# The sparse and the stick-breaking attention take their four query blocks from the last to the first

## The chip, the cores and the metric

The kernel runs on one core of one Trainium2 chip, as one launch. The metric is device time in microseconds (us). Engines are named as the profile names them: PE is TensorE's matrix unit, PEld its weight load, DVE VectorE, ACT ScalarE, POOL GpSimd, SP the queue that issues the weight loads from memory.

## The reference, cut to what matters

Two stacks of two transformer layers run one after the other over 512 tokens of width 1024. The second stack is the one concerned. Each of its layers mixes tokens in three ways, projects the joined result back to width 1024, and goes through a feed-forward part.

```
o_gdn = gated_deltanet(...)                 # a scan over chunks of 64 tokens
o_nsa = native_sparse_attention(...)        # 6 heads: compressed + selected + window
o_sb  = stick_breaking_attention(q, k, v)   # 4 heads
mix = concat([o_gdn, norm(o_nsa), norm(o_sb)])
h = h + mix @ w_out
```

Both attentions are causal and run over four query blocks of 128 tokens. Block b sees the keys of blocks 0 to b, so its score tiles are 128(b+1) wide: block 0 has the smallest tiles, block 3 the largest. The blocks don't depend on each other. With 512 tokens all eight selection blocks of 64 keys are chosen and the window reaches back over everything, so the selected and the windowed part are both plain causal attention, over different keys and values. In the stick-breaking attention a weight is sigmoid(z) times the product of sigmoid(-z) over the keys behind it.

## The kernel before, in words

All products of a projection are made of three fp32r products (high x high, high x low, low x high), so PE carries far more than any other engine. A weight tile comes from memory on SP's queue (L266), ACT copies its high part (`whi`, L278) and DVE subtracts (`wlo`, L279).

Inside a mixing stage `drive` fixes PE's order by hand while the program is built. One generator, `main`, makes the projections. Side generators (`spawn`, `begin`, `crew`) make everything else. Each yields the time, on a planned clock that counts PE's columns, at which its next products may stand; a priority and a share decide who goes next. Every product is then chained to the one before it, so PE keeps this order whatever happens on the chip. The other engines' order comes from a scheduler that places instructions by a timeline of its own. Each engine then runs its list in order.

What matters for the change, in `block2_mix`:

- `nsa` yields jobs in an order given by its loop over b: `compressed(b)`, then 6 heads on the selected keys (`vs`), then 6 heads on the window (`vw`). A crew of 4 workers (`LIVE[2]`) takes them one by one.
- A head (`head`, L705 on) is: score products (`k`,`kl` with `q`, and the causal mask) into a PSUM bank; maximum `nm` on DVE; exponential `e` on ACT; transposes of `e` on PE; a copy `et` on ACT or DVE; products with the values into `ps_o`.
- After 6 heads `add_part` scales the sum (`no`, DVE) and adds it on POOL (`on`). After the third part `head_norm` follows: square `hsq` on ACT, a sum and a scale `hv` on DVE, a power on POOL, the product `on` on DVE.
- When the crew is through, `mark("nsa")` stands 8.62 planned us later. Then `mix_features` transposes `on` (12 transposes) and splits it into `hi` (ACT) and `lo` (DVE), which gives `mix1`.
- `main` goes on meanwhile with the projections `z1`, `sq`, `sk`, `sv`, and then waits for `mix0` (from the delta-rule scan) and `mix1` before `out_proj(mixa)`, 144 products of 512 columns.
- `breaking` turns `sq` and `sk` into transposed halves: 8 + 8 transposes, 4 copies `q` and 8 copies `k` on ACT, as many subtractions `q` and `kl` on DVE. It then starts `stick`, a crew of 4 over four blocks of 4 heads. A head there is scores, two sigmoids `sn` and `sg` on ACT, a scan `rest` on DVE, a product `sg` on DVE, transposes, `et`, products with `sv`.
- In the first layer of the stack `main` also broadcasts a scale (`dgh`, `dgl`, `rb`) at the same spot.

```
for b in range(4):                       # L1909, nsa
    yield compressed(b)
...
for b in range(4):                       # L1978, stick
```

Of the kernel before, what the change touches and what calls it, by code (L numbers as in the profile page):

```python
# [289 lines left out]
def build(ctx, tc, a, out, off, stages=99):  # L290
# [24 lines left out]
    def tmp(shape, name, tag="tmp", dt=F):  # L315
        return slot.tile(shape, dt, tag=tag, name=name, bufs=BUFS[tag])

    def ty(shape, name):
        return tiny.tile(shape, F, tag=f"ty{int(np.prod(shape[1:]))}", name=name)
# [16 lines left out]
    def act(out, in_, func=ACTF.Copy, **kw):  # L336
        ins = nc.scalar.activation(out=out, in_=in_, func=func, **kw).ins  # L337
        kind = SETS.get(func)
        if kind is None:
            return  # L340
        if kind != run_["set"]:
            run_["before"] = [i.name for i in run_["now"]]
            run_["set"], run_["now"], run_["first"] = kind, [], ins
            for name in run_["before"]:
                tc.add_manual_dep(ins, name, NOSYNC, reason="one table set after another")
        else:
            tc.add_manual_dep(ins, run_["first"].name, NOSYNC, reason="one table set after another")
        run_["now"].append(ins)

    def tt(out, in0, in1, op):  # L350
        return nc.vector.tensor_tensor(out=out, in0=in0, in1=in1, op=op)  # L351
# [4 lines left out]
    def ts(out, in0, s1, s2=None, op0=ALU.mult, op1=None):  # L356
        if s2 is None:
            return nc.vector.tensor_scalar(out=out, in0=in0, scalar1=s1, scalar2=None, op0=op0)
        return nc.vector.tensor_scalar(out=out, in0=in0, scalar1=s1, scalar2=s2, op0=op0, op1=op1)
# [43 lines left out]
    def mark(name, lag=0.0):  # L403
        marks[name] = pe["t"] + lag
# [253 lines left out]
    def heads(t, h):  # L658
        return t.rearrange("p (h d) -> p h d", h=h)
# [41 lines left out]
    def scores(q, k, i, b, n):  # L701

        return tuple((q[i][:, blk(b)], part[i][:, 0:n]) for part in k)

    def head(b, weigh, v, out, lag):  # L705

        yield after(0, "s")
        e = weigh()
        yield after(lag[0] + lag[1] * b, "t")
        tp = ps("t", 1.2 + 0.3 * b)  # L710
        for j in range(b + 1):
            tr(tp[:, blk(j)], e[:, blk(j)])
        et = tmp([128, 128 * (b + 1)], "et")
        nc.any.tensor_copy(out=et, in_=tp[:, 0:128 * (b + 1)])
        yield lag[2] + lag[3] * b
        room = after(0, "o")
        yield lambda: room() or not out.fresh()
        o, done = out()
        for j in range(b + 1):
            mm_narrow(o, et[:, blk(j)], v(j), j == 0, j == b)  # L720
        done()
        yield

    def softmax(b, qk, ssum, mask=None):

        n = 128 * (b + 1)
        sp = ps("s", 1.6 + 0.6 * b)
        for i, (q, k) in enumerate(qk):
            mm(sp[:, 0:n], q, k, i == 0, False)
        if mask is None:  # L730
            mm(sp[:, blk(b)], identb, trib, False, True)
        else:
            mm(sp[:, 0:n], identb, mask, False, True)
        nm = ty([128, 1], "nm")
        reduce(nm, sp[:, 0:n], ALU.max, negate=True)
        e = tmp([128, n], "e")
        act(e, sp[:, 0:n], ACTF.Exp, bias=nm, accum_out=ssum)
        return e

    def group(n, finish):  # L740

        st = {"left": n}

        def place(i):
            def out():
                if st["left"] == n:
                    st["o"] = ps("o", np.inf)
                    st["room"] = rooms["o"][-1]
                st["left"] -= 1
                return st["o"][:, 64 * i:64 * i + 64], last if st["left"] == 0 else lambda: None  # L750

            out.fresh = lambda: st["left"] == n
            return out

        def last():
            finish(st["o"])
            st["room"][0] = pe["t"] + 1.5

        return [place(i) for i in range(n)]
# [570 lines left out]
    def block2_mix(l, st, nxt, shared):  # L1330
# [529 lines left out]
        def add_part(b, o, factor):  # L1860
            o, factor = heads(o[:, 0:384], 6), factor.unsqueeze(2).to_broadcast([128, 6, 64])
            if on[b] is None:
                on[b] = sl([128, 6, 64], "on")
                tt(on[b], o, factor, ALU.mult)
            else:
                t = tmp([128, 6, 64], "no")
                tt(t, o, factor, ALU.mult)
                gt(on[b], on[b], t, ALU.add)
            parts[b] += 1
            if parts[b] == 3:  # L1870
                tt(on[b], on[b], head_norm(on[b], 6), ALU.mult)
# [34 lines left out]
            yield  # L1906

        def nsa():
            for b in range(4):  # L1909
                yield compressed(b)  # L1910
                for c, (kk, v) in enumerate(((kh["ks"], vs), (kh["kw"], vw))):
                    ssum = ty([128, 6], "ssum6")

                    def finish(o, b=b, c=c, ssum=ssum):
                        ts(ssum, ssum, 1e-30, op0=ALU.max)
                        nc.vector.reciprocal(out=ssum, in_=ssum)
                        tt(ssum, ssum, sig[:, b, 6 * c + 6:6 * c + 12], ALU.mult)
                        with tc.high_priority():
                            add_part(b, o, ssum)

                    for i2, out in enumerate(group(6, finish)):
                        zz = slice(64 * (i2 % 2), 64 * (i2 % 2) + 64)
                        yield head(b, lambda b=b, i2=i2, kk=kk, ssum=ssum: softmax(b, scores(nqh[i2 // 2], kk, i2 % 2, b, 128 * (b + 1)), ssum[:, i2:i2 + 1]),
                                   lambda jj, v=v, zz=zz: v[:, jj, zz], out, LAG[2])
            mark("nsa_weights")

        def sparse():
            yield until("ks", "kw", "nq0", "nq1", "nq2", "vs", "cmp_k", "cmp_v")
            crew(LIVE[2], nsa(), "nsa", lag=8.62)
            yield until("nsa")  # L1930
            yield from mix_features(on, 1)
# [43 lines left out]
            return sg  # L1975

        def stick():
            for b in range(4):  # L1978
                def finish(o, b=b):
                    t = tmp([128, 4, 64], "sbt")  # L1980
                    act(t, heads(o[:, 0:256], 4))
                    tt(heads(ob[b], 4), t, head_norm(t, 4), ALU.mult)

                for h, out in enumerate(group(4, finish)):
                    yield head(b, lambda b=b, h=h: weigh(b, h), lambda jj, h=h: sv[h // 2][:, jj, 64 * (h % 2):64 * (h % 2) + 64], out, LAG[3])
# [211 lines left out]
```

## Time and profile before

| | us |
|---|---|
| median of 3 runs | 3046.4 |
| the runs | 3045.38, 3050.75, 3046.40 |
| the profiled execution | 3048.71 |
| its span on the core | 3046.9 |
| PE busy in it | 2961.4 (97%) |

The profiled execution lies 2.3 us above the median, and its span 1.8 us below its own time. All times of day below are us from the start of the span. The two mixing stages of the second stack, where the change lies, run from about 1360 to 1780 and from about 2210 to 2620. The sparse attention runs there from 1546 to 1680 in the first of these layers, and ends at 2522 in the second; the stick-breaking attention follows it.

### The profile page before, as it was taken

How to read it: one execution, taken by the hardware profiler on the slowest of the kernel's cores; microseconds unless marked ns; L12 is line 12 of the kernel's file. 1: busy time of each engine (PE TensorE's matmuls, PEld its weight loads, DVE VectorE, ACT ScalarE, POOL GpSimd, SP SyncE). 2: the span in 40 equal slices, each digit the busy share in tenths (PEclk: the TensorE clock that was granted, in tenths of full speed). 3: DMA queues.
4: the chain of work that ended last, by engine and by line, in shares of the span. 5: the costliest groups of instructions: out<-in, count | busy, mean ns of one | idle time of the engine just before them, and what ended most of it. 6: DMA issues, size and time to landing. Idle time of an engine off the chain costs nothing.

```text
span 3046.9 us, 46920 instructions
## 1 busy us (share of the span) xinstructions
PE 2961.4 (97%) x18306; PEld 2471.1 (81%) x18306; DVE 1884.5 (62%) x3426; ACT 1362.9 (45%) x2542; POOL 714.9 (23%) x874
## 2 busy tenths in 40 slices
PE   8999999999999999999999999999999998999998
PEld 7888788888887888888888778887788987788876
DVE  6858444447858434457866675555678666755556
ACT  5654422234645422245455553335454565433353
POOL 4211311123201311145313120002454131200024
PEclk9999999999999999999999999999999999999999
DMA  3212333332222333332310222232323102222322
GB/s 130 82 45 68 90 95 93 96 118 85 68 71 74 96 97 92 95 120 73 94 54 21 81 91 91 95 106 90 116 77 84 63 24 80 92 92 95 106 90 76
DMA packets 105791, 259.38 MB, mean 85 GB/s; under 512 B 21728, under 2 KB 40033, under 8 KB 105569
## 3 DMA queue, kind: packets, MB, share of 16 engines
q1 hardware_dynamic: 97504, 241.70, 25.6%
q10 hardware_dynamic: 8064, 14.68, 1.4%
q8 instruction: 144, 2.36, 0.3%
q14 instruction: 79, 0.64, 0.1%
HBM read 242.84 MB, written 13.50 MB: 84 GB/s over the span
## 4 chain that ended last, share of the span: by engine, by line
PE 45%; DVE 5%; ACT 2%; issue 1%; POOL 1%; DMA 1%; SPq 0%; DVEq 0%; ACTq 0%; POOLq 0%
PE ps_g L382 36%; PE ps_s L382 5%; PE ps_s L392 2%; PE ps_o L388 2%; DVE wlo L279 1%; DVE conv L362 1%; PE ps_s L388 1%; POOL ru L354 1%; ACT whi L278 1%; DVE kl L351 0%; DVE inv L365 0%; ACT L337 0%; DVE pr L351 0%; DVE lo L362 0%; DVE x L351 0%
## 5 line engine op out<-in xcount | busy, mean ns | idle before, releaser
L382 PE MATMUL ps_g<-hi,whi 128*128 128x512 f32 x2768 | 1097.5, 397 | 9.4 <-DVE x L351 3.9
L382 PE MATMUL ps_g<-lo,whi 128*128 128x512 f32 x2768 | 1094.4, 395 | 6.4 <-DVE lo L362 5.8
L382 PE MATMUL ps_g<-hi,wlo 128*128 128x512 f32 x2768 | 1095.5, 396 | 0.0
L278 ACT ACTIVATE whi<-wraw 128x1024 fp32r<-128x1024 f32 (+3 forms) x442 | 458.0, 1036 | 863.3 <-PE ps_g L382 609.5
L279 DVE TENSOR_TENSOR wlo<-wraw,whi 128x1024 fp32r<-128x1024 f32 (+3 forms) x442 | 547.0, 1238 | 252.1 <-ACT whi L278 249.1
L382 PEld LDWEIGHTS ps_g<-hi,whi 128*128 128x128 f32 x2768 | 522.1, 189 | 132.8 <-DVE x L351 6.0
L382 PEld LDWEIGHTS ps_g<-lo,whi 128*128 128x128 f32 x2768 | 522.7, 189 | 127.8 <-DVE lo L362 7.5
L382 PEld LDWEIGHTS ps_g<-hi,wlo 128*128 128x128 f32 x2768 | 522.0, 189 | 115.1
L382 PE MATMUL ps_g<-whi,hi 128*128 128x256 f32 (+4 forms) x1232 | 379.3, 310 | 10.0 <-ACT whi L278 9.1
L382 PE MATMUL ps_g<-whi,lo 128*128 128x256 f32 (+4 forms) x1232 | 347.2, 284 | 3.2 <-DVE lo L362 3.2
L382 PE MATMUL ps_g<-wlo,hi 128*128 128x256 f32 (+4 forms) x1232 | 347.2, 284 | 0.7 <-DVE wlo L279 0.7
L382 PEld LDWEIGHTS ps_g<-whi,hi 128*128 128x128 f32 (+1 forms) x1232 | 232.7, 189 | 26.5 <-ACT whi L278 9.5
L382 PEld LDWEIGHTS ps_g<-whi,lo 128*128 128x128 f32 (+1 forms) x1232 | 231.3, 188 | 5.8 <-DVE lo L362 4.2
L382 PEld LDWEIGHTS ps_g<-wlo,hi 128*128 128x128 f32 (+1 forms) x1232 | 232.5, 189 | 2.6 <-DVE wlo L279 1.0
L354 POOL TENSOR_TENSOR sq<-sq 128x512 f32<-128x512 f32 x102 | 159.9, 1567 | 266.8 <-ACT sq L337 247.9
L354 POOL TENSOR_TENSOR relu<-relu 128x512 f32<-128x512 f32 x64 | 100.9, 1577 | 506.5 <-ACT relu L337 506.5
L362 DVE SCALAR_TENSOR_TENSOR conv<-cv,small,conv 128x512 f32<-128x512 f32 x230 | 186.8, 816 | 5.8 <-ACT conv L337 2.3
L351 DVE TENSOR_TENSOR cv<-ps_g,rb 128x512 f32<-128x512 f32 x106 | 72.8, 690 | 142.8 <-PE ps_g L382 142.7
L351 DVE TENSOR_TENSOR x<-ps_g,x 128x512 f32<-128x512 f32 x112 | 76.9, 688 | 131.6 <-PE ps_g L382 130.9
L337 ACT ACTIVATE e<-ps_s,nm 128x128 f32<-128x128 f32 (+3 forms) x192 | 100.5, 526 | 106.3 <-DVE nm L365 103.2
L351 DVE TENSOR_TENSOR ff<-ps_g,rb 128x512 f32<-128x512 f32 x64 | 44.3, 692 | 162.8 <-PE ps_g L382 162.8
L365 DVE TENSOR_REDUCE nm<-ps_s 128x1 f32<-128x128 f32 (+3 forms) x192 | 91.8, 486 | 80.9 <-PE ps_s L382 78.9
(435 smaller groups left out, 3622.5 us busy)
## 6 DMA issues: line engine op xcount, KB each, us to landing
wraw<-in_w_ff SPq DMA_DIRECT2D x128, 512.0 KB, 3.6
wraw<-in_w_up SPq DMA_DIRECT2D x88, 512.0 KB, 3.4
wraw<-in_w_down SPq DMA_DIRECT2D x32, 448.0 KB, 3.2
wraw<-in_w_out SPq DMA_DIRECT2D x20, 512.0 KB, 3.7
wraw<-in_w_g SPq DMA_DIRECT2D x18, 512.0 KB, 3.5
wraw<-in_w_down SPq DMA_DIRECT2D x16, 512.0 KB, 3.4
wraw<-in_w_pg SPq DMA_DIRECT2D x16, 512.0 KB, 3.4
wraw<-in_w_cq SPq DMA_DIRECT2D x12, 512.0 KB, 3.4
```

What stands on the lines that cost most here:

```text
L278: self.nc.scalar.activation(out=hi, in_=t, func=ACTF.Copy)
L279: self.nc.vector.tensor_tensor(out=lo, in0=t, in1=hi, op=ALU.subtract)
L337: ins = nc.scalar.activation(out=out, in_=in_, func=func, **kw).ins
L351: return nc.vector.tensor_tensor(out=out, in0=in0, in1=in1, op=op)
L354: return nc.gpsimd.tensor_tensor(out=out, in0=in0, in1=in1, op=op)
L362: return nc.vector.scalar_tensor_tensor(out=out, in0=in0, scalar=scalar, in1=in1, op0=op0, op1=op1)
L365: return nc.vector.tensor_reduce(out=out, in_=in_, axis=AX.X, op=op, negate=negate)
L382: placed(nc.tensor.matmul(out=out, lhsT=lhsT, rhs=rhs, start=start, stop=stop).ins, n)
L388: placed(nc.tensor.matmul(out=out[z], lhsT=lhsT[:, z], rhs=rhs, start=start, stop=stop).ins, n)
L392: placed(nc.tensor.transpose(out=out, in_=in_, identity=ident[0:n, 0:n]).ins, 256)
```

## The change

Both loops over the query blocks run 3, 2, 1, 0 instead of 0, 1, 2, 3. Nothing else is edited. The same instructions are issued on each engine, with the same shapes; since PE's order and the other engines' lists are made from the order of the jobs, about 1,100 rows of PE's list stand otherwise in each of the two layers.

```diff
         def nsa():
-            for b in range(4):
+
+            for b in (3, 2, 1, 0):
                 yield compressed(b)
...
         def stick():
-            for b in range(4):
+
+            for b in (3, 2, 1, 0):
                 def finish(o, b=b):
```

Place 1: PE at the end of the sparse attention, first layer of the stack. `ps_g<-whi,hi` and its two neighbours are products of a projection, `ps_g<-hi,whi` those of `out_proj`, `vw,et` the last step of a head of the window part, `on` the transposes that `out_proj` waits for. Before, from the last projection product on (24 such products stand between the last head and the broadcast):

```order
L382 MATMUL ps_g<-whi,hi 128x256
L382 MATMUL ps_g<-wlo,hi 128x256
L382 MATMUL ps_g<-whi,lo 128x256
L382 MATMUL ps_s<-dgh,ones_r 128x512
L382 MATMUL ps_s<-dgl,ones_r 128x512
L392 MATMUL ps_s<-const_105,sq 128x128 x8
L392 MATMUL ps_s<-const_105,sk 128x128 x8
L392 MATMUL ps_s<-const_105,on 128x128 x12
L382 MATMUL ps_g<-hi,whi 128x512
L382 MATMUL ps_g<-lo,whi 128x512
L382 MATMUL ps_g<-hi,wlo 128x512
```

Now, again from the last projection product on:

```order
L382 MATMUL ps_g<-whi,lo 128x256
L392 MATMUL ps_s<-const_105,e 128x128
L382 MATMUL ps_s<-dgh,ones_r 128x512
L382 MATMUL ps_s<-dgl,ones_r 128x512
L392 MATMUL ps_s<-const_105,sq 128x128 x8
L392 MATMUL ps_s<-const_105,sk 128x128 x8
L388 MATMUL ps_o<-vw,et 64x64 x2
L382 MATMUL ps_s<-k,q 128x128
L382 MATMUL ps_s<-kl,q 128x128
L382 LDWEIGHTS identb
L382 MATMUL ps_s<-mskb,identb 128x128
L388 MATMUL ps_o<-vw,et 64x64 x2
```

The projections now end before the sparse attention does. Behind these rows follow the transposes and value products of the heads of block 0 that are still open (6 value steps and 2 scores in all), then the scores of the first four stick-breaking heads (8 products of 512 columns), the 12 transposes of `on`, 8 transposes of `sg`, three products of `out_proj`, 4 more transposes of `sg`, and the first product with `sv`. In the second layer it stands the same way, without the broadcast and with 9 products of `out_proj` ahead of the first product with `sv`.

Place 2: ACT at the same spot (`sv` is the last copy out of a projection, `q` and `k` the copies of the transposed halves). Before:

```order
L337 ACTIVATE sv<-ps_g,rmix 128x128 x4
L337 ACTIVATE hsq<-on 128x384
L337 ACTIVATE dgh<-const_105,rf 128x128 x4
L337 ACTIVATE sv<-ps_g,rmix 128x128
L278 ACTIVATE whi<-wraw 128x768
L337 ACTIVATE sv<-ps_g,rmix 128x128 x3
L337 ACTIVATE rb<-ps_s 128x512
L337 ACTIVATE q<-ps_s 64x512 x4
L337 ACTIVATE k<-ps_s 64x512 x8
```

Now:

```order
L337 ACTIVATE sv<-ps_g,rmix 128x128
L278 ACTIVATE whi<-wraw 128x768
L337 ACTIVATE sv<-ps_g,rmix 128x128 x3
L337 ACTIVATE dgh<-const_105,rf 128x128 x4
L337 ACTIVATE rb<-ps_s 128x512
L337 ACTIVATE q<-ps_s 64x512 x4
L337 ACTIVATE k<-ps_s 64x512 x4
L337 ACTIVATE e,ssum_17010<-ps_s,nm 128x128
L714 COPY et<-ps_s 128x128
L337 ACTIVATE k<-ps_s 64x512 x4
L337 ACTIVATE e,ssum_17010<-ps_s,nm 128x128
L714 COPY et<-ps_s 128x128 x2
```

The exponentials and copies of the last heads now stand among and behind the copies `q` and `k`, and the broadcast's `dgh` behind the last `sv`. After these rows come `hsq`, a load of the sigmoid's table, and the eight sigmoids of the first four stick-breaking heads.

Place 3: DVE at the same spot (`rest` is the scan, `lo` the last step of `mix_features`). Before:

```order
L351 TENSOR_TENSOR no<-ps_o,ssum_16828 128x384
L365 TENSOR_REDUCE hv<-hsq 128x6
L362 SCALAR_TENSOR_TENSOR dgl<-const_105,rf,dgh 128x128 x2
L359 TENSOR_SCALAR hv<-hv 128x6
L362 SCALAR_TENSOR_TENSOR dgl<-const_105,rf,dgh 128x128 x2
L279 TENSOR_TENSOR wlo<-wraw,whi 128x768
L351 TENSOR_TENSOR on<-on,hv 128x384
L351 TENSOR_TENSOR q<-ps_s,q 64x512 x4
L351 TENSOR_TENSOR kl<-ps_s,k 64x512 x8
L362 SCALAR_TENSOR_TENSOR lo<-ps_s,small_12853,hi 128x512 x3
```

Now (the `q` and `kl`, with two `nm` of the last heads between and behind them, stand ahead of these rows):

```order
L365 TENSOR_REDUCE hv<-hsq 128x6
L1974 SCALAR_TENSOR_TENSOR rest<-sn 128x512
L359 TENSOR_SCALAR hv<-hv 128x6
L351 TENSOR_TENSOR sg<-sg,rest 128x512
L1974 SCALAR_TENSOR_TENSOR rest<-sn 128x512 x2
L351 TENSOR_TENSOR sg<-sg,rest 128x512
L351 TENSOR_TENSOR on<-on,hv 128x384
L351 TENSOR_TENSOR sg<-sg,rest 128x512
L1974 SCALAR_TENSOR_TENSOR rest<-sn 128x512
L351 TENSOR_TENSOR sg<-sg,rest 128x512
L362 SCALAR_TENSOR_TENSOR lo<-ps_s,small_12853,hi 128x512 x3
L714 COPY et<-ps_s 128x512 x3
```

The work of the widest stick-breaking block now stands inside the chain from `hv` over `on` to `lo`; before, `on` came right behind that chain's start and the stick-breaking scans came after `lo`.

## Rows read from the trace of the kernel before

**Rows 1.** The page's busy times: engine, busy us, share of the span, instructions.

```profile
PE 2961.4 (97%) x18306; PEld 2471.1 (81%) x18306; DVE 1884.5 (62%) x3426; ACT 1362.9 (45%) x2542; POOL 714.9 (23%) x874
```

**Rows 2.** Windows: length, busy us by engine (instructions), granted clock, DMA share, GB/s.

```profile
1540.00:1560.00 20.00, 18.68 (x162) 17.35 (x163) 11.53 (x30) 11.17 (x37) 0.00 (x0) 1.00 0.17 53
...
1680.00:1700.00 20.00, 14.27 (x75) 11.70 (x75) 15.85 (x28) 13.38 (x29) 2.37 (x2) 0.81 0.38 125
1700.00:1720.00 20.00, 19.25 (x101) 15.35 (x102) 14.49 (x31) 9.92 (x30) 1.99 (x9) 0.85 0.18 49
2520.00:2540.00 20.00, 13.15 (x102) 11.18 (x100) 13.04 (x20) 12.37 (x25) 2.34 (x2) 0.97 0.44 137
2540.00:2560.00 20.00, 19.40 (x135) 15.31 (x133) 11.49 (x26) 11.25 (x33) 1.98 (x9) 0.94 0.21 68
```

**Rows 3.** Timeline, PE, first layer's joint: start, duration, instruction, idle before and releaser.

```profile
1679.15 0.69 PE L388 MATMUL ps_o<-vw,et 128*64 128x64 f32 x16
...
1683.38 0.50 PE L382 MATMUL ps_s<-dgh,ones_r 128*128 128x512 f32 x1 [0.51 <-ACT dgh L337]
...
1686.00 0.60 PE L392 MATMUL ps_s<-const,on 128*128 128x128 f32 x4
...
1696.77 0.79 PE L382 MATMUL ps_g<-lo,whi 128*128 128x512 f32 x1 [2.77 <-DVE lo L362]
```

**Rows 4.** Timeline of the same joint, ACT, DVE and POOL.

```profile
1679.26 1.14 ACT L337 ACTIVATE sv<-ps_g,rmix 128x128 f32<-128x128 f32 x4 [1.57 <-PE ps_g L382]
...
1679.89 0.56 DVE L351 TENSOR_TENSOR no<-ps_o,ssum 128x384 f32<-128x384 f32 x1 [3.63 <-PE ps_o L388]
...
1681.63 0.53 ACT L337 ACTIVATE hsq<-on 128x384 f32<-128x384 f32 x1 [1.23 <-POOL on L354]
...
1682.06 1.26 ACT L337 ACTIVATE dgh<-const,rf 128x128 fp32r<-128x128 f32 x4
...
1683.42 1.36 POOL L354 TENSOR_TENSOR hv<-hv,mhalf 128x6 f32<-128x6 f32 x1 [1.83 <-DVE hv L359]
...
1683.48 0.83 ACT L278 ACTIVATE whi<-wraw 128x768 fp32r<-128x768 f32 x1
...
1685.22 0.55 DVE L351 TENSOR_TENSOR on<-on,hv 128x384 f32<-128x384 f32 x1
...
1685.44 2.42 ACT L337 ACTIVATE q<-ps_s 64x512 fp32r<-64x512 f32 x4
...
1687.89 4.23 ACT L337 ACTIVATE k<-ps_s 64x512 fp32r<-64x512 f32 x7
...
1690.33 5.60 DVE L351 TENSOR_TENSOR kl<-ps_s,k 64x512 fp32r<-64x512 f32 x8 [0.84 <-ACT k L337]
...
1695.96 2.07 DVE L362 SCALAR_TENSOR_TENSOR lo<-ps_s,small,hi 128x512 fp32r<-128x512 f32 x3
```

**Rows 5.** Groups by form, 1545 to 1765: count, busy us, mean ns, idle before.

```profile
L1973 DVE TENSOR_TENSOR_SCAN rest<-sn 128x512 f32<-128x512 f32 x4 | 4.9, 1220 | 0.1
...
L337 ACT ACTIVATE e<-ps_s,nm 128x128 f32<-128x128 f32 x12 | 4.4, 365 | 3.1 <-DVE nm L365 3.1
...
L351 DVE TENSOR_TENSOR sg<-sg,rest 128x512 f32<-128x512 f32 x4 | 2.6, 682 | 0.4 <-ACT sg L337 0.4
L337 ACT ACT_TABLE_LOAD x2 | 2.6, 1283 | 5.2 <-PE ps_s L382 5.2
...
L337 ACT ACTIVATE sn<-ps_s 128x512 f32<-128x512 f32 x4 | 2.5, 619 | 0.0
...
L714 DVE COPY et<-ps_s 128x512 f32<-128x512 f32 x3 | 2.0, 680 | 0.0
```

**Rows 6.** Timeline, PE: steps of a head of block 0, then of block 3.

```profile
1553.15 0.34 PE L388 MATMUL ps_o<-vs,et 128*64 128x64 f32 x4
...
1654.18 0.40 PE L382 MATMUL ps_s<-k,q 128*128 128x512 f32 x1
1654.42 0.39 PE L382 MATMUL ps_s<-kl,q 128*128 128x512 f32 x1
```

## The prediction

> **What bounds the kernel now.** I read the page first: PE is busy 97% of the span [rows 1], and no instruction is added or removed. PE's work is a constant, then, and the time can only move by what PE waits and by the clock it gets. So I read PE's busy time and granted clock in windows over the two mixing stages that the change reorders. Two spots stand out, one per layer, both where the sparse attention ends and the stick-breaking attention begins; I call them the joints. In the first layer PE stands 20.00 - 14.27 = 5.7 us in 1680 to 1700, in the second 20.00 - 13.15 = 6.9 us in 2520 to 2540 [rows 2]. The granted clock falls there too: 0.81 and 0.85 in the two windows of the first joint, 0.97 and 0.94 in the second, so stretches run at the lower of the two levels (1.2 GHz) after PE has stood.
>
> Then the timeline of the first joint. The last head's value products begin at 1679.15, and projection products cover PE until 0.51 us before the broadcast [rows 3], that is until 1682.87. Beside them runs the chain from the last head: `no` at 1679.89, the square, the power on POOL, `on` done at 1685.77 [rows 4], 5.9 us in all. It is ready before PE reaches the transposes of `on` at 1686.00 [rows 3]. What PE waits for is DVE: the last wait, 2.77 us, ends with `lo`, which starts only when `kl` is through (1690.33 + 5.60) [rows 3, 4]. So before, the end of the sparse attention is covered by projections, and the halves of `sk` are what comes last.
>
> **The change: the joint of the first layer.** The rows of place 1 say that the cover is gone: the projections run out while two heads of block 0 have still to get their scores. I count from the end of the last projection product, t = 0, by the new order and the old durations.
>
> - ACT (place 2): `sv` x4 1.14, `whi` 0.83, `dgh` x4 1.26 [rows 4], with 0.2 for hand-overs: `dgh` is there at 3.4. PE waits, since `dgh` stands in its list ahead of the rest.
> - From `dgh` on PE to the end of `kl` on DVE took 1695.93 - 1683.38 = 12.55 [rows 3, 4]; the copies `q` and `k` on ACT and `q` and `kl` on DVE are the same now. So 3.4 + 12.55 = 15.9. The last head's `nm` stands behind `kl`, its `e` (0.37) [rows 5] behind that, then a transpose, a copy and its value product (0.34) [rows 6], with `nm` at some 0.3: the last head ends at about 17.6, `no` starts at 17.9.
> - The chain to `on` is longer (place 3). `hsq` ended 2.3 after the start of `no` [rows 4]: 20.1. Then the table load 1.28, `sn` 0.62, the scan 1.22 [rows 5]: 23.3. Only then comes the small step of `hv`, 0.2, and POOL's 1.36 [rows 4]: 25.0. Meanwhile DVE has one `sg`, two scans, another `sg`, from 23.5: 0.68 + 2 x 1.22 + 0.68 = 3.8, so `on` runs from 27.3 to 27.9, 10.0 after `no` instead of 5.9.
> - Behind it on DVE: `sg`, scan, `sg` 2.6, `lo` x3 2.07 [rows 4], `et` 0.68 [rows 5]. PE's first product with `sv` waits for that `et`: 33.3.
> - PE's work before that point: `dgh` to the end of `sk`, 1686.00 - 1683.38 = 2.6 [rows 3]; some 13 small steps of block 0 at 0.3 or so, 4.0 [rows 6]; four heads' scores at twice 0.24 and a mask, 2.2 [rows 6]; 12 transposes of `on` and 12 of `sg` at 0.11 each (8 of `sq` and 8 of `sk` fit into the 2.6), 2.6; three products at 0.24, 0.7. Sum 12.1.
>
> PE stands 33.3 - 12.1 = 21.2, where it stood 5.7: **+15.5**.
>
> **The joint of the second layer.** No broadcast. ACT: `sv` 1.14, `whi` 0.83 and 0.3 for hand-overs [rows 4], so the first `q` starts at 2.3. DVE's `kl` began 1690.33 - 1685.44 = 4.9 after ACT's first `q` and took 5.60 [rows 4]; now a copy and a small step stand among them, 0.5: they end at 13.3, and after two more small steps `no` starts at 13.6. The last head isn't later than that here, since its `nm` and `e` stand ahead of half of `k` and `kl`. The same 10.0 to the end of `on`: 23.6. Then 2.6 + 2.07 + 0.68: 29.0. PE's work before that: 1.8 for `sq` and `sk`, 4.0, 2.2, 28 transposes 3.1, nine products 2.2: 13.3. It stands 15.7 instead of 6.9: **+8.8**.
>
> **The rest, costed at nothing, with bounds.** The start of the sparse attention now has wide heads with projection products between them; the 1.3 us that PE stands in 1540 to 1560 [rows 2] may go or double (-1.3 to +1.3). In blocks 1 and 0 three heads go in step with short covers, and in the first layer DVE has 8 products `x` ahead of the scans of the stick-breaking block 2: between nothing and 4 us. I let these cancel. Later in both stages some 80 to 90 products of `out_proj` are left when the last stick-breaking block is through, where some 50 were; either covers `mixb`, so nothing is lost or gained at that end. The weight loads on SP keep their order.
>
> The clock: rows 2 show what the old joints lose, 20 x (0.19 + 0.15) = 6.8 and 20 x (0.03 + 0.06) = 1.8, part of it while PE stood. Longer waits will not lower that, but most of a longer wait costs nothing at a lower clock. I take no change, between -4 (part of 8.6) and +5 (the second layer becoming like the first). The Trainium skill ("TensorE: Matmul & The Clock Gate", HAM oscillation) says that an engine which waits again and again starts the next stretch at the half clock; by it the second joint would cost as the first, and the sum would be 5 higher, which the range holds. The trace agrees in kind: both joints fall below 1.00, to 0.81 and to 0.94 [rows 2].
>
> The table load of the sigmoid lies inside the chain now; I price it at 1.28 [rows 5]. The Trainium skill ("ScalarE: Activation LUTs", What ACT_TABLE_LOAD costs) adds a drain of about 1.4 to each switch; by it each chain would be that much longer and the sum 2.8 higher. Nothing in the rows shows such a drain.
>
> **Sum.** 15.5 + 8.8 = +24.3 on the profiled execution's own 3048.7, that is 3073.0. That execution lay 2.3 above the median of the runs, so I predict 3046.4 + 24.3 = **3071**.
>
> Low end of this case: if DVE's scans cost the chain nothing (as when the scheduler's order were harmless: `on` 5.9 after `no`, `lo` at once), each joint ends 4.1 + 2.6 = 6.7 earlier: 24.3 - 13.4 = +10.9; with -4 for the clock and -1.3 at the start, +5.6: 3052. High end: +24.3, +5 clock, +4 in the rest, and 8 for waits on PSUM banks that I did not follow: +41, 3088.
>
> **Rivals.** (1) *Faster: the small blocks make a short tail.* A head of block 0 is short (0.37 for its exponential [rows 5]), and the halves of `sq` and `sk` are now made before `on`, so the 2.77 us wait for `lo` behind `kl` [rows 3] falls away. If the last heads got through ACT and DVE ahead of `k` and `kl`, both joints would vanish with their clock: -5.7 - 6.9 and up to -8.6, say 3046 - 15 = 3031. It decides where the last value product comes less than about 3 us after the projections end. For it: everything after `on` is smaller. Against it: places 2 and 3, where the last `nm` stands behind 12 steps `q` and `kl`. 7%.
>
> (2) *No change.* Work that moves into the joint (scores, transposes of `sg`) fills it, and the start of the stage gives back what is lost: 3046, within 6. Against it: the filler I counted, 12 us, is already in the sum. 8%.
>
> (3) *Worse: DVE becomes the bound through the stick-breaking stage.* Block 3's four scans and products (4 x 1.90 [rows 5]), the `x` products (8 at 0.69, as a `lo` of that shape [rows 4]) and block 2's scans stand at the front, where DVE is already late; each block then waits for it: another 4 to 6 us a block in both layers, some 20 more, 3092. Against it: PE has 15 to 21 products of `out_proj` (3.5 to 4.9 us) ahead of block 2's transposes, and the rest of the stage is light. 8%.
>
> My forecast has 77%. A measurement here tells about 0.2% (6 us) from no change. **Faster 7%, same 9%** (rival 2 and the lowest end of the forecast), **slower 84%**. The range 3051 to 3090 is the forecast's own, stretched at the top into rival 3; it leaves out rivals 1 and 2, part of 3, and the forecast's edges.
>
> **What would show it.** Right: PE's windows at both joints with 15 to 21 us idle between the last projection product and the first product with `sv`, the largest waits named `dgh` (first layer), `e`, `on` and `et`; `on` some 10 us after its `no`, with scans between the two steps of `hv`; elsewhere PE as full as before. Wrong: `on` within 6 us of the end of the projections (rival 1); joints as short as before (rival 2); or idle spread over the whole stick-breaking stage (rival 3).

## The result and the profile after

The changed kernel takes **3071.2 us** (median of 6 runs, 3069.89 to 3080.29) against 3049.4 us for the kernel before on the same chip (6 runs): a ratio of **1.0082**, 95% interval 1.0071 to 1.0092. (The ratio is formed over the runs; the quotient of the two medians is 1.0071.) The forecast was 3071 us, "slower". The total is right; two of its terms are not, as the profile shows. That it was met to 0.2 us is luck: the forecast stood on a median of 3046.4 us for the kernel before, which is 3049.4 here, and the added time is 21.8 us where 24.3 was forecast.

The profiled execution of the changed kernel took 3070.06 us, its span is 3068.3 us. The page's busy times, to be held against [rows 1]:

```profile
PE 2970.5 (97%) x18304; PEld 2475.7 (81%) x18306; DVE 1888.8 (62%) x3438; ACT 1358.9 (44%) x2530; POOL 714.3 (23%) x874
```

The span grew by 21.4 us, and PE's busy time by 9.1 of them, though PE has the same products to do. So only 12.3 us are added idle time; the rest is products that took longer, at a lower clock. The counts of DVE and ACT correct the section on the change in one point: twelve copies `et` have moved from ACT to DVE (3426 to 3438 instructions and 2542 to 2530), so that not quite the same instructions are issued on each engine.

Windows of the changed kernel around the two joints (columns as in [rows 2]):

```profile
1540.00:1560.00 20.00, 19.25 (x152) 17.01 (x153) 9.91 (x21) 10.24 (x25) 0.00 (x0) 0.91 0.11 36
...
1680.00:1700.00 20.00, 12.41 (x59) 8.98 (x60) 12.58 (x25) 11.71 (x29) 1.00 (x1) 0.61 0.06 20
1700.00:1720.00 20.00, 14.79 (x119) 11.35 (x118) 17.39 (x25) 9.39 (x17) 2.20 (x5) 0.79 0.32 106
...
2540.00:2560.00 20.00, 8.51 (x37) 5.49 (x37) 14.58 (x25) 10.58 (x22) 2.58 (x5) 0.62 0.00 1
2560.00:2580.00 20.00, 20.00 (x176) 15.88 (x176) 14.00 (x23) 8.04 (x17) 2.07 (x6) 0.96 0.38 125
```

Both joints are longer, and the granted clock in them is 0.61 to 0.79 where it was 0.81 and 0.85 in the first layer, and 0.62 and 0.96 where it was 0.97 and 0.94 in the second [rows 2].

To see what each layer loses, I take one window per layer from the same instruction ahead of the sparse attention to the same instruction behind the stick-breaking attention (a matrix update and a `lo` of the feed-forward on DVE in the first layer; a rotation of `nq` and such a `lo` in the second). The kernel before:

```profile
1531.40:1808.95 277.55, 265.25 (x2279) 222.85 (x2278) 185.22 (x365) 155.45 (x385) 66.75 (x91) 0.98 0.19 58
2364.10:2646.73 282.63, 272.38 (x2400) 231.40 (x2399) 191.03 (x384) 160.46 (x394) 64.39 (x87) 0.99 0.19 61
```

The changed kernel:

```profile
1528.10:1818.77 290.67, 271.42 (x2280) 225.95 (x2278) 188.50 (x370) 154.24 (x380) 66.12 (x91) 0.95 0.18 56
2375.00:2668.24 293.24, 276.42 (x2400) 234.03 (x2399) 191.44 (x390) 158.10 (x387) 62.64 (x87) 0.97 0.18 59
```

The first layer's stage grew by 290.67 - 277.55 = **13.1 us**, of them 19.25 - 12.30 = 6.9 idle and 6.2 longer products; the second's by **10.6 us**, 6.6 idle and 4.0 longer products. That is 23.7 us for both. The span shows 21.4 because this execution reached the first stage 3.3 us earlier, which is a difference between executions (e1, with the same sparse order, reached it at 1532.30), and lost 1.1 us between the two stages.

Timeline of the first layer's joint in the changed kernel, PE (to be held against [rows 3]; the first row is the last projection product):

```profile
1678.56 0.29 PE L382 MATMUL ps_g<-whi,lo 128*128 128x256 f32 x1
...
1681.96 0.79 PE L382 MATMUL ps_s<-dgh,ones_r 128*128 128x512 f32 x1 [3.01 <-ACT dgh L337]
...
1691.88 0.45 PE L382 MATMUL ps_s<-k,q 128*128 128x128 f32 x1 [1.95 <-DVE kl L351]
...
1694.81 0.45 PE L392 MATMUL ps_s<-const,e 128*128 128x128 f32 x1 [2.14 <-DVE kl L351]
...
1707.10 2.82 PE L392 MATMUL ps_s<-const,on 128*128 128x128 f32 x12 [5.21 <-DVE on L351]
...
1712.83 0.69 PE L388 MATMUL ps_o<-sv,et 128*64 128x64 f32 x16
```

The other engines in the same stretch (to be held against [rows 4]):

```profile
1688.94 5.72 DVE L351 TENSOR_TENSOR kl<-ps_s,k 64x512 fp32r<-64x512 f32 x8 [0.23 <-ACT k L337]
...
1697.52 0.56 DVE L351 TENSOR_TENSOR no<-ps_o,ssum 128x384 f32<-128x384 f32 x1 [1.35 <-PE ps_o L388]
...
1699.79 1.28 ACT L337 ACT_TABLE_LOAD   x1
...
1701.09 0.60 ACT L337 ACTIVATE sn<-ps_s 128x512 f32<-128x512 f32 x1
...
1701.71 1.22 DVE L1974 TENSOR_TENSOR_SCAN rest<-sn 128x512 f32<-128x512 f32 x1 [1.35 <-ACT sn L337]
...
1703.08 1.85 POOL L354 TENSOR_TENSOR hv<-hv,mhalf 128x6 f32<-128x6 f32 x1 [3.86 <-DVE hv L359]
...
1706.49 0.54 DVE L351 TENSOR_TENSOR on<-on,hv 128x384 f32<-128x384 f32 x1
```

In the order of time: `dgh` is late, `kl` holds up the last sparse heads, `no` comes at 1697.52 instead of 1679.89 [rows 4], and the chain to `on` runs with the table load and a wide scan in it. The largest waits of PE in the second layer's stage are of the same kind:

```profile
PE ps_s L392 <- DVE on L351: 5.9, 1, 5.9
PE ps_o L388 <- DVE et L714: 3.5, 1, 3.5
PE ps_s L392 <- DVE kl L351: 2.1, 1, 2.1
```

### The profile page after: what moved, and what is told of

Read it like the earlier page. It is cut to its first block, busy times and chain, and to the rows that moved or that the text cites. A ratio compares the mean times of both kernels' runs of the same rounds, so it can differ in the third digit from the quotient of the medians.

```text
span 3068.3 us, 46928 instructions
## 1 busy us (share of the span) xinstructions
PE 2970.5 (97%) x18304; PEld 2475.7 (81%) x18306; DVE 1888.8 (62%) x3438; ACT 1358.9 (44%) x2530; POOL 714.3 (23%) x874
## 4 chain that ended last, share of the span: by engine, by line
PE 45%; DVE 5%; ACT 2%; issue 1%; POOL 1%; DMA 1%; SPq 0%; DVEq 0%; ACTq 0%; POOLq 0%
PE ps_g L382 36%; PE ps_s L382 5%; PE ps_s L392 2%; PE ps_o L388 2%; DVE conv L362 1%; DVE wlo L279 1%; PE ps_s L388 1%; POOL ru L354 0%; DVE kl L351 0%; ACT whi L278 0%; DVE inv L365 0%; DVE pr L351 0%; DMA lsc<-L 0%; ACT L337 0%; DMA ll<-lsc 0%
## 5 line engine op out<-in xcount | busy, mean ns | idle before, releaser
L2032 POOL MEMSET cv<- 128x2 f32 x88 | 8.7, 99 | 557.3 <-DVE conv L362 555.5
```

Source lines behind the costliest of these rows:

```text
L2032: nc.gpsimd.memset(h[:, 0:2], 0.0)
```

## The experiments

Ratios are to the kernel before, timed on the same chip beside each set; "us over" is the difference of the two medians. The ratio is formed over all runs, so the two need not agree to the last digit.

| run | what | us | us over | ratio, 95% interval |
|---|---|---|---|---|
| e1 | sparse order reversed alone | 3071.8 | +23.9 | 1.0078 (1.0065 to 1.0090) |
| e2 | stick-breaking order reversed alone | 3054.1 | +6.2 | 1.0020 (1.0010 to 1.0029) |
| e3 | both, share 0.24 | 3068.8 | +20.9 | 1.0066 (1.0054 to 1.0079) |
| e4 | both, 40 added products a layer | 3069.4 | +21.4 | 1.0072 (1.0057 to 1.0088) |
| e5 | both, rising share | 3053.4 | +6.1 | 1.0019 (1.0010 to 1.0028) |
| e6 | old order, halves earlier | 3058.2 | +10.9 | 1.0037 (1.0024 to 1.0049) |
| e7 | both, halves earlier | 3076.4 | +29.1 | 1.0098 (1.0085 to 1.0112) |
| e8 | both, rising share, halves earlier | 3068.2 | +21.0 | 1.0070 (1.0057 to 1.0082) |
| e9 | sparse order reversed alone, rising share | 3050.1 | +3.6 | 1.0012 (1.0003 to 1.0020) |
| e10 | old order, share 0.24 | 3063.4 | +16.9 | 1.0062 (1.0048 to 1.0076) |
| e11 | old order, falling share | 3055.3 | +7.4 | 1.0020 (1.0011 to 1.0029) |
| e12 | old order, share 0.15 beside block 3 | 3053.0 | +5.1 | 1.0010 (1.0000 to 1.0020) |

### Which order costs it: e1 and e2

e1 has the first of the two edits alone, e2 the second.

```diff
 # e1: in nsa()
-            for b in range(4):
+            for b in (3, 2, 1, 0):
 # e2: the same in stick()
```

> Only the sparse attention goes from the last block to the first; the stick-breaking attention keeps its order. Theory (the cover of projection products is gone at the joints because the sparse attention now ends in short heads): nearly the whole loss is here, 14 to 19 us over the kernel before, a little less than with both orders reversed, since the first stick-breaking block is narrow: its two scans and products in the chain to `on` take 0.42 us each instead of 1.22, so `on` comes about 2.7 us earlier and the first product with `sv` about 5.8 us earlier than in the changed kernel, and some 2.8 us less of PE's work lies in between. Rival A (the stick-breaking order does it: its wide scans stand in the chain): within 5 us of the kernel before. Rival B (short heads cost something wherever they stand, not at the joint alone): as slow as the changed kernel, 20 us or more.

> Only the stick-breaking attention goes from the last block to the first. Theory: the projections still cover the end of the sparse attention, and `on` is ready before PE comes to it, so the joint keeps its idle time of some 6 to 7 us and the time stays within 4 us of the kernel before. Rival A: 8 to 16 us slower, with the wait for the first product with `sv` behind four wide scans. Rival B: a few us slower, with idle time at the end of the stick-breaking stage.

e1 loses 23.9 us, as much as both edits, so the sparse order is enough for the whole loss. I had expected 14 to 19, since narrow scans leave the chain; the number is that of rival B (20 or more), which e9 below decides. The wide scans do leave it: the transposes of `on` come 21.9 us behind the broadcast's `dgh` instead of 25.1, and PE's longest wait for `on` is shorter. But another wait follows. PE's waits in e1, first layer's stage:

```profile
PE ps_s L392 <- DVE on L351: 4.5, 1, 4.5
PE ps_s L392 <- DVE sg L351: 3.9, 2, 2.1
PE ps_s L382 <- ACT dgh L337: 3.0, 1, 3.0
...
PE ps_s L392 <- DVE kl L351: 2.1, 1, 2.1
PE ps_s L382 <- DVE kl L351: 1.9, 1, 1.9
```

Behind the joint the narrow stick-breaking heads leave PE too little to do and it waits for `sg`; in e1's window 1720 to 1740 PE is busy 16.88 us at a clock of 0.83, where the changed kernel has 20.00 us. So the wide scans in the chain to `on` are not needed for the loss: without them it is as large, with another wait in their place.

e2 loses 6.2 us, a little over the 4 that I allowed, and the two losses do not add up: 23.9 + 6.2 is 8 us more than both edits cost together. Its trace shows a wait that the kernel before does not have at that place. PE's waits for `sg` in e2, first layer's stage:

```profile
PE ps_s L392 <- DVE sg L351: 4.1, 3, 3.1
```

The longest, 3.1 us up to 1711.73, is that of the transposes of the widest block, which now comes right behind the joint. In the second layer the same wait is 1.9 us, where no wait for `sg` was over 0.6 before; PE's idle time in that stage is none the larger for it (9.7 against 10.3 us), but its products take 5.6 us longer (277.9 against 272.4).

### Is it the missing cover: e3, e4, e5 and e9

e3 lowers the projections' share of PE throughout the sparse attention, so that more of them are left at the joint.

```diff
-    SHARE = (0.42, 0.42, 0.71, 0.3, 0.43)
+    SHARE = (0.42, 0.42, 0.71, 0.24, 0.43)
```

> Both orders reversed as in the changed kernel, and the share of PE that the projections get beside the sparse attention (SHARE[3]) cut from 0.3 to 0.24, so that 60 projection products are left behind the last head's value product, and 33 products of out_proj stand between `on` and the first stick-breaking scores. Theory (lost cover): the loss is given back, within 5 us of the kernel before, both joints at under 7 us of idle time and a granted clock of 0.9 or more. Rival A (wide scans in the chain): 8 to 13 us slower still. Rival B (short heads cost anywhere): 15 us slower or more.

e4 adds work to the changed kernel where the projections end.

```diff
+        for i in range(10):
+            p = ps("g")
+            for j in range(4):
+                mm(p, kh["kw"][0][0][:, blk(0)], kh["kw"][0][0])
+            yield
         begin(breaking())
```

> The changed kernel with 40 added products of 128x512 a layer behind the last projection, on operands that lie there, whose results nobody reads. At 0.235 us each they are 9.4 us of PE's work a layer, 18.8 in all. Theory (PE stands and slows down at the joints for want of work that it could do): the added work is free or better, 0 to 15 us below the changed kernel, and the granted clock at the joints rises to 0.85 or more. Rival (PE's own work sets the time, or the chain at the joint is only pushed back by what is added): 15 to 19 us above the changed kernel.

e4 is as my theory has it: some 18.8 us of added work, and the time is 3069.4, not above the changed kernel's 3071.2 (21.4 and 21.8 us over the kernel before, each on its own chip). Windows of e4, PE alone (length, busy, granted clock), over the joints:

```profile
1680.00:1720.00 40.00, 33.19 (x165) 0.91 0.25 83
2520.00:2560.00 40.00, 34.19 (x223) 0.96 0.22 69
```

The changed kernel had 12.41 + 14.79 = 27.2 us of work in the first of these, at 0.61 and 0.79. By the pages, PE's busy time in e4 is only 8.9 us above that of the changed kernel with 18.8 us more to do (2979.4 against 2970.5): the other 9.9 us came back, with the granted clock of the run at 0.990 instead of 0.985. PE's idle time fell from 97.8 to 86.8 us, and the kernel before has 85.5 (3046.9 - 2961.4): the added work fills what the changed kernel loses.

e3, though, misses: it gives back 1 us or so, and rival B's number (15 or more) came out. Its first joint is cured (PE busy 13.13 of 20 us at a clock of 0.91 in 1680 to 1700, close to the kernel before), but in both layers a new wait stands at the end of the stick-breaking stage:

```profile
PE ps_s L392 <- DVE sbo L351: 3.8, 1, 3.8
```

As I read it, the products of `out_proj` that now fill the joint are missing there. PE also stands more in the middle of the sparse attention (17.91 of 20 us busy in 1580 to 1600, where the changed kernel has 20.00). The two layers differ, in the same windows from the matrix update or the rotation to the `lo` as above:

```profile
1527.96:1812.90 284.94, 265.04 (x2279) 222.03 (x2277) 187.15 (x371) 154.35 (x379) 64.64 (x91) 0.98 0.17 57
2368.45:2666.60 298.15, 279.50 (x2399) 236.79 (x2398) 189.44 (x383) 161.02 (x392) 65.53 (x87) 0.97 0.18 58
```

e3 takes 5.7 us less than the changed kernel in the first layer and 4.9 us more in the second, so it is not the clean test of the joint that I meant it to be. So I changed the theory: the products of the projections and of `out_proj` are a fixed stock of cover, and the question is beside which heads they are spent. Wide heads give one another cover; short ones do not. e5 keeps both reversed orders and lets the share rise as the heads get shorter; e9 does so with the sparse order alone reversed.

```diff
-    SHARE = (0.42, 0.42, 0.71, 0.3, 0.43)
+    SHARE = (0.42, 0.42, 0.71, 0.22, 0.43)
...
             for b in (3, 2, 1, 0):
+                if b == 2:
+                    share(0.25)
+                if b == 1:
+                    share(0.3)
+                if b == 0:
+                    share(0.5)
                 yield compressed(b)
```

> Both orders reversed, and the share of the projections beside the sparse attention rises with the blocks: 0.22 while block 3 runs, then 0.25, 0.3 and 0.5 for block 0. 18 to 24 projection products are left behind the last value product, and 12 products of out_proj stand ahead of the first stick-breaking scores, about as with only the stick-breaking order reversed (15). Theory now (the products are a fixed stock of cover; the changed order spends them beside wide heads, which cover one another, and e3 kept some for the joint but spent products of out_proj there): 4 to 10 us over the kernel before, near the run with only the stick-breaking order reversed, and no wait for `sbo` over 2 us at the end of the stage. Rival (short heads at the end of the sparse attention lose it wherever the cover stands, and e3 shows it): 16 to 22 us over the kernel before.

> The sparse attention from the last block to the first with the rising share of e5, the stick-breaking attention in its old order: e1 with the cover put back. Theory (what the reversed sparse order costs is the cover it spends too early, and the 6 us of e2 and e5 belong to the stick-breaking order): within 4 us of the kernel before, 20 us or more below e1. Rival (the reversed sparse order has a price of its own, and e5 only by chance equals e2): 5 to 12 us over the kernel before.

Both hold: e5 is 6.1 us over the kernel before and has no wait for `sbo` among those of PE, e9 is 3.6 us over it and 20 us below e1. In e9 the waits of the first joint are again those of the kernel before, `lo` with 2.8 us and `q` with 2.4, and `dgh` has 1.2 where e1 has 3.0. So rival B falls: the short heads at the end do not cost e1's loss by themselves. e5's one larger wait in the first layer is that of e2, 3.2 us for `sg`, which e9 does not have. Windows of 40 us for the projection and `out_proj` products alone (tile `ps_g`, PE: length, busy and, in brackets, the number of products, clock) show what was moved. The kernel before:

```profile
1540.00:1580.00 40.00, 13.44 (x84) 1.00 0.13 41
1580.00:1620.00 40.00, 18.28 (x93) 1.00 0.07 21
1620.00:1660.00 40.00, 18.60 (x98) 1.00 0.06 18
1660.00:1700.00 40.00, 19.87 (x101) 0.91 0.24 81
```

The changed kernel:

```profile
1540.00:1580.00 40.00, 15.50 (x78) 0.96 0.10 32
1580.00:1620.00 40.00, 18.80 (x96) 1.00 0.08 25
1620.00:1660.00 40.00, 20.06 (x116) 1.00 0.07 21
1660.00:1700.00 40.00, 8.72 (x57) 0.81 0.07 21
```

e5:

```profile
1540.00:1580.00 40.00, 8.77 (x55) 1.00 0.09 27
1580.00:1620.00 40.00, 15.99 (x81) 1.00 0.10 28
1620.00:1660.00 40.00, 18.59 (x111) 1.00 0.07 21
1660.00:1700.00 40.00, 22.53 (x120) 0.96 0.23 68
```

The counts are safer to compare than the busy times, which grow where the clock is low (0.96 in the changed kernel's first window). In the first 120 us, beside blocks 3 to 1, the changed kernel issues 290 of these products, the kernel before 275 and e5 247. Around the joint the changed kernel has 57 left instead of 101, and e5 has 120. The changed kernel runs 3.3 us ahead in these windows, which moves a few products from one to the next and not such differences.

### Are the copies to blame: e6, e7 and e8

In these the stick-breaking thread begins ahead of the projections of `sq`, `sk` and `sv`, so that the copies `q`, `k` and `kl` are made beside later projections and not at the joint; e6 in the old order, e7 with both orders reversed, e8 with e5's share besides.

```diff
+        begin(breaking())
         for name, sc in (("sq", r8), ("sk", r), ("sv", r)):
...
-        begin(breaking())
```

> The kernel before, in its own order, with the stick-breaking thread begun ahead of the projections of `sq`, `sk` and `sv`, so that the halves of `sq` and `sk` (the copies `q`, `k`, `kl`) are made beside the later projections and not at the joint. Theory (at the joint of the kernel before PE waits for `q`, `kl` and for `lo` behind them): those waits go, 5 to 6 us a layer with the clock that they cost; the products of out_proj stay for later; 6 to 14 us faster. Rival (cover is a fixed stock: with the copies gone the wait is only taken by the last sparse head's chain to `on` and the broadcast, since no work is left in the joint): within 4 us of the kernel before.

> The changed kernel with the same earlier begin of the stick-breaking thread: the 5.6 us of `kl` and the copies `q` and `k` no longer stand ahead of the last sparse heads on ACT and DVE at the joint. Theory (the chain at the changed joint is `dgh`, then the copies, then the last heads, then `on`): the chain from the last projection product to the first product with `sv` falls from 34 and 30 us to some 22, PE's own work there falls by 2 to 3 us: 8 to 20 us below the changed kernel. Rival (the short heads' own latency and the scans set the joint, the copies lie beside them): within 5 us of the changed kernel.

> Both together: orders reversed, the rising share of e5 and the earlier halves of e6. Theory: the joint has its cover and no copies: below e5 by 4 to 14 us, so between 8 us faster and 4 us slower than the kernel before. Rival (cover is a fixed stock, and the joint takes what is missing): within 3 us of e5.

All three miss: each is slower than its counterpart without the edit, by 10.9 us (e6 against the kernel before) and 14.8 us (e8 against e5, 3068.2 - 3053.4), and e7 by 5 to 7 us against the changed kernel (3076.4 against 3071.2 us; 29.1 against 21.8 over the kernel before), where I had expected 8 to 20 us less. e6 and e8 lie outside their rivals' ranges as well. PE's waits in e6, first layer's stage, where before `q` (2.4 us) and `lo` (2.8 us, [rows 3]) were the largest:

```profile
PE ps_s L382 <- DVE kl L351: 4.1, 2, 3.0
PE ps_s L382 <- ACT dgh L337: 3.5, 1, 3.5
PE ps_s L392 <- DVE sg L351: 2.0, 2, 1.7
```

The copies are as long elsewhere as at the joint: earlier, they stand on DVE in front of sparse heads, which wait for them, and in e6's first layer only 3 projection products are left behind the last value product, where 24 were, so that PE waits 3.5 us for `dgh` instead of 0.51 [rows 3]. So the copies are one link of the chain at the joint, but not one that can be taken out by making them sooner.

### Is there something better than both: e10, e11 and e12

If cover is a stock, the old order might gain by keeping some for its own joints. e10 sets 0.24 for the whole sparse attention; e11 and e12 keep the cover beside the short blocks and save it beside the wide ones.

```diff
 # e10
-    SHARE = (0.42, 0.42, 0.71, 0.3, 0.43)
+    SHARE = (0.42, 0.42, 0.71, 0.24, 0.43)
 # e11: 0.32 in SHARE, and in nsa(), ahead of compressed(b)
+                if b == 2:
+                    share(0.25)
+                if b == 3:
+                    share(0.2)
 # e12: 0.3 in SHARE, and
+                if b == 3:
+                    share(0.15)
```

> The kernel before in its own order with SHARE[3] cut from 0.3 to 0.24: the transposes of `on` now come ahead of the last 21 and 18 projection products, so that 51 products of out_proj stand between the transposes of `sk` and the first stick-breaking scores, where 15 and 12 stood behind `on`. Theory (a fixed stock of cover, to be put where the waits are): the waits of the joint for `q` and `lo` shrink from 5.7 and 6.9 us to under 3; what is lost is cover beside the first, short blocks of the sparse attention and at the end of the stick-breaking stage, whose last heads are wide: between 10 us faster and 3 us slower. Rival (the end of the stage needs those products, as in e3, where PE then waited 3.8 us for `sbo` in each layer): 5 to 15 us slower.

> The kernel before in its own order, with a share that falls: 0.32 beside blocks 0 and 1, 0.25 beside block 2, 0.2 beside block 3, whose wide heads cover one another. 27 and 54 projection products are left behind the last value product (24 before), and 18 and 27 products of out_proj behind `on` (15 and 12 before). Theory (fixed stock of cover, to be put where the waits are): short heads keep their cover, unlike in e10, and the joint gets more: 1 to 8 us faster than the kernel before. Rival (the order of the kernel before has no cover to spare: the joint's waits for `q` and `lo` are set by the copies on ACT and DVE whatever lies ahead of them): within 3 us of it, or slower by up to 6 us with PE waiting at the end of the stage.

> The same with one step: 0.3 as before, then 0.15 beside block 3. In the first layer 61 projection products are left behind the last value product, so that the transposes of `on` come ahead of those of `sk`, and `lo` of the mix can come ahead of `kl` on DVE; 45 products of out_proj then lie beside the copies. Theory: the wait for `lo` goes in the first layer (2.8 us and the clock behind it), little changes in the second: 2 to 7 us faster than the kernel before. Rival (as in e10, what is spent at the joint is missing at the stage's end): 2 to 8 us slower.

None is faster than the kernel before: +16.9, +7.4 and +5.1 us, the last with an interval that begins at 1.0000. In e10 the waits for `q` and `lo` are gone from the joint, as expected, but larger ones take their place. PE's waits in e10, first layer's stage:

```profile
PE ps_g L382 <- DVE x L351: 8.9, 2, 6.9
PE ps_s L392 <- ACT e L337: 2.9, 1, 2.9
PE ps_s L392 <- DVE sbo L351: 2.6, 1, 2.6
```

The wait for `sbo` is the one that the rival names. The longest, however, stands at the joint itself:

```profile
1699.16 1.29 DVE L351 TENSOR_TENSOR x<-ps_g,x 128x512 f32<-128x512 f32 x2
...
1699.90 0.79 PE L382 MATMUL ps_g<-hi,whi 128*128 128x512 f32 x1 [6.92 <-DVE x L351]
```

In each layer 36 products of `out_proj` run in e10's joint, and the next one waits, 6.9 and 5.0 us, until DVE, which has `q` and `kl` and more to do first, adds the first finished result to `x`. So the products of `out_proj` cover the joint only as far as DVE can take their results away. e11 keeps the waits for `q` and `lo` (2.4 and 2.6 us in the first layer), as its rival has it; e12 loses the one for `lo` there and gets waits for `sg`, `sbo` and `x` of 2.0 to 2.7 us. No version here beats the kernel before.

## Why the prediction was right, and where it was not

- **The cover is gone: right.** e1, e5 and e9 show it from both sides: the sparse order alone gives the loss, and the same order with the cover put beside the short heads gives 16 to 20 us of it back. The trace names the place: from the last projection product the changed joint runs to the first product with `sv` without any projection product.
- **The chain of the first joint: right to about a microsecond.** From the end of the last projection product (1678.85): `dgh` on PE 3.1 (forecast 3.4), `kl` through 15.8 (15.9), `no` 18.7 (17.9), the scan through 24.1 (23.3), POOL 26.1 (25.0; its step took 1.85 instead of 1.36), `on` through 28.2 (27.9), the first product with `sv` 34.0 (33.3).
- **The chain of the second joint: right, 2 us short.** From 2533.86: `kl` 12.7 (13.3), `no` 14.2 (13.6), `on` 24.1 (23.6), the first product with `sv` 31.2 (29.0).
- **The idle time was too large, and the clock term, taken as no change, was too small.** These two windows run from the last projection product to the first product with `sv` in the changed kernel:

```profile
1678.85:1712.83 33.98, 20.13 (x92) 15.09 (x92) 24.12 (x41) 20.02 (x43) 3.68 (x7) 0.65 0.09 28
2533.86:2565.07 31.21, 17.15 (x100) 12.75 (x97) 23.52 (x39) 17.95 (x36) 3.06 (x7) 0.73 0.13 40
```

PE stands 33.98 - 20.13 = 13.9 us and 31.21 - 17.15 = 14.1 us, where I had 21.2 and 15.7. The work between them takes 20.1 and 17.2 us, where I had counted 12.1 and 13.3 at the full clock. A mean clock of 0.65 and 0.73 says that 70% and 54% of these stretches (twice what is missing to 1.00, there being two levels) ran at 1.2 GHz. So the failed step is the sentence "Longer waits will not lower that, but most of a longer wait costs nothing at a lower clock. I take no change": the waits lowered the clock from 0.81 and 0.85 to 0.61 and 0.79, and in the second layer from 0.97 and 0.94 to 0.62 and 0.96; with work put into the waits (e4) it was 0.91 and 0.96 over 40 us. Since the chain on ACT, DVE and POOL sets how long a joint is, slower products of PE filled part of the waits and did not come on top. Over the whole stages my +15.5 and +8.8 of idle time and nothing for the clock came out as +6.9 and +6.6 of idle time and +6.2 and +4.0 of longer products: 24.3 against 23.7. The sum is near because both errors are one: the same microseconds were put under waiting. That it comes this near is luck: the first layer lost 2.4 us less than its term and the second 1.8 more, and up to 1.8 us of the first layer's longer products are not the joint's (see the rest, below).

The Trainium skill ("TensorE: Matmul & The Clock Gate", HAM oscillation) says that an engine which waits again and again starts the next stretch at the half clock, and by it the second joint should become like the first. The trace agrees: the mean clock is 0.73 over the second joint and 0.65 over the first, and the second stage has 4.0 us of longer products.

- **The scans in the chain: a wrong low end.** I had held that without DVE's scans each joint would end 6.7 us earlier and the loss fall to 10.9. e1 has only narrow scans there and loses 23.9: the wait for `on` falls only from 5.2 to 4.5 us, and waits for `sg` of 3.9 us and a window at 0.83 come behind it.
- **The waits' names: `on`, `dgh` and `et` as forecast, `e` not.** In its place PE waited twice for `kl` (1.95 and 2.14 us in the first joint). The exponential that the second wait's transpose reads had ended at 1689.30, 5.5 us before. Of the eight `kl` the fourth ends at 1691.73 and the eighth at 1694.66, each the last reader of one of the two banks with the transposes of `sk`; PE's two waits end 0.15 us behind them, and the products that waited read nothing that these `kl` write. What `kl` gave free was therefore most likely the PSUM bank. I had named such waits only as 8 us at the high end.
- **The rest, costed at nothing: not quite.** At the start of the sparse attention PE's wait is 1.5 us where it was 1.3 (it begins ahead of 1540 here), and the clock in 1540 to 1560 is 0.91 instead of 1.00, 1.8 us. That dip is not shown to be the change's: e1 and e4, with the same sparse order, have 1.00 there. Behind the first joint nothing was lost: 20.00, 19.83 and 18.19 us busy in 1720 to 1780 against 19.82, 19.56 and 17.88 before.
- **The table load: right at its own 1.28.** `sn` starts at 1701.09, 0.02 us after the load ends. The Trainium skill ("ScalarE: Activation LUTs", What ACT_TABLE_LOAD costs) adds a drain of about 1.4 to each switch. The rows show none: the load begins 0.02 us after `hsq` ends (1699.77), and `sn` as soon after the load.
- **The rivals.** Faster (a short tail): fell, since the last `nm` did stand behind `kl`. No change: fell, since the work that moved into the joints left PE 13.9 and 14.1 us idle. DVE as the bound of the whole stick-breaking stage: fell, by the windows of 1720 to 1780.

Open: why e3's one low share costs 15 us more than e5's rising one is shown only by its new waits and by its second layer; no run takes them away one by one. Each call of `share` also starts its count of used time anew, which no run takes apart from the new value. That the waits for `kl` are waits for a bank was not tried alone either. Of what the reversed stick-breaking order costs by itself (about 6 us in e2) the wait for `sg` is seen, and its longer products in the second layer are not explained.

## What to carry to other kernels

Products that wait for nothing are a stock of cover for the engine that bounds the kernel, as far as somebody takes their results away (e10); when an order of blocks is turned round, look at where the rule that spends this stock now spends it. Here more beside the short blocks and less beside the wide ones took the reversed sparse order from 3071.8 (e1) to 3050.1 us (e9). In the old order, where the short blocks come first, the same rule gained nothing over one share for all (e11 and e12, 7 and 5 us slower by the medians), so it is not shown beyond this case. Where the other engines set the length of a joint, count its length, not PE's idle time: waits and products slowed by the clock share the same microseconds, and added work there can be free (e4). A copy that is moved to an earlier place still stands in somebody's queue (e6 to e8).

## What the runs showed that I had not expected

- 18.8 us of added products cost nothing and 9.9 us of other products' time came back with the clock: mean granted clock of the run 0.990 with them, 0.985 without.
- Small differences in the place of the cover are worth nearly as much as the change itself: old order, one share from 0.30 to 0.24, +16.9 us (e10).
- The costs of the two reversed orders do not add: 23.9 and 6.2 us alone, 21.8 us together.
